# First steps of a hybrid decoder layer rearranged: weight blocks loaded ahead, a PSUM bank for each channel block, small loads on other queues

## The chip, the cores and the metric

One core of one Trainium2 chip runs the whole layer as one program. The metric is the device time of one execution in microseconds (us), lower is better. The kernel before the change takes 423.1 us (median of three runs, 421.59 to 423.76).

## What is computed

One decoder layer on 256 tokens of 1024 channels, all in float32. RWKV-7 time mixing and block attention run side by side on the same normalised input, which one combined projection `w_in` (1024 x 5408) feeds; then gates, an output projection, and a gated MLP with a causal convolution.

```python
h = rms_norm(x, norm1_g[l])
proj = h @ w_in[l]
z_rwkv, z_moba, gate_pre = ...            # 1824, 1536 and 2048 columns
z_rwkv = z_rwkv + rwkv_mu[l] * (shift_right(z_rwkv) - z_rwkv)
# inside rwkv7_time_mix:
w_log = -softplus(-(decay_bias + tanh(xw) @ w_decay_up)) - 0.5
a = sigmoid(aaa_bias + xa @ w_aaa_up)
...                                       # scan over the tokens, attention
x = x + (g_a * (y_a @ w_branch_a[l]) + g_b * (y_b @ w_branch_b[l])) @ w_out[l]
h2 = rms_norm(x, norm2_g[l])
x = x + conv_ffn(h2, w_ffn_up[l], ffn_conv_w[l], ffn_conv_b[l], w_ffn_down[l])
```

## The kernel before

**Products in three parts.** Each float32 matrix is held as a high half (`whi`, `hh`) and a remainder (`wlo`, `hl`), and a product is high x high, high x low and low x high. Weights come from memory in blocks of 512 KB: a DMA on SP's queue fills a buffer `raw`, a cast makes `whi`, a subtraction on DVE makes `wlo`. There are four `raw` buffers (`NRAW`), four of `whi` and three of `wlo`. A new block is loaded when the block four places earlier has been split (`load_next` in `split_lo`).

**The order of the work.** The first steps, function `first_steps`, stand in the order in which they are written (`manual_schedule`); what comes after is placed by a scheduler on each engine's queue. On an engine, instructions run strictly in that order. The blocks are called b0, b1, ... here, by their place in the load order: b0 and b1 are the 256 columns from 1536 on (they hold the inputs `xwa` and `xg` of the decay and gate paths), b2 the last 128 columns of that part, b3 and b4 the first half of the key projection, b5 and b6 its second half, and so on.

**The first steps.** ACT squares x, DVE scales it (`xn`), PE turns it into channel blocks by transposes into the PSUM tiles `xt`; two channel blocks share a PSUM bank. ACT takes the high half `hh` of each of the eight channel blocks (`high`), DVE the remainder `hl` (`low`). DVE casts b0, GpSimd (POOL) subtracts it, ACT casts b1 to b3, and DVE casts b4, b5 and b6. PE takes the products of b0 and b1 block by block (lines L408, L412). GpSimd issues 19 small loads (`small_loads`: parameter rows `p1`, `p2`, the matrices `wdu`, `wgu`). Between stages `keep_warm` issues products whose result nobody reads.

**The decay path.** After b0 and b1, ACT and DVE shift the result (`xwa`, L428 and L429, with the parameters `omm`), ACT takes the tanh (L447), and PE multiplies it by `wdu` into the tiles `at` and `ch` (L499), in a fixed place of its queue between the products of the projection (L266, L268 high, L271 low halves). From there a long chain of small steps leads to the transposes `prx` (L550), which need the ACT copy `rx` (L540).

**The end.** The last MLP block is added to four PSUM banks `fin[0]` to `fin[3]`, a quarter of the result each; DVE scales each and adds x (L1220), SP stores it. The last quarter goes in two halves, which both lie in `fin[3]`.

**Completion counters.** Loads issued on the queues of SP and ACT take eight completion counters in turn, `DMAHW0` to `DMAHW7`; those of GpSimd take eight others. In the lists below `[waits DMAHW3_49]` at a DMA that fills a buffer for the first time means that it is not issued until the load that used this counter last has landed.

Of the kernel before, what the change touches and what calls it, by code (L numbers as in the profile page):

```python
# [36 lines left out]
def body(tc, x, positions, norm1_g, w_in, rwkv_mu, w_decay_up, decay_bias, w_aaa_up,  # L37
# [5 lines left out]
    with ctx:  # L43
# [36 lines left out]
        def load_x():  # L80
            xs = []
            for t in range(2):
                xt = b4("x").rearrange("p a b -> p (a b)")
                for cs in (slice(0, 512), slice(512, 1024)):
                    nc.sync.dma_start(xt[:, cs], xr[t * 128:(t + 1) * 128, cs])
                xs.append(xt)
            return xs
# [6 lines left out]
        p1 = t1("p1", (51, 128))  # L94
        p2 = t1("p2", (88, 128))
# [3 lines left out]
        x_sb = load_x()  # L99
        AR = b8("AR", [128, 16, 2, 64])  # L100
        ones = cst.tile([128, 512], mybir.dt.bfloat16, name="ones")
        idle = acc("idle")

        def keep_warm(n):

            for _ in range(n):
                pe.matmul(idle, ones[:, 0:128], ones, start=True, stop=True)

# [26 lines left out]
        par = cst.tile([128, 59], F32, name="par")  # L135
        cpar = cst.tile([128, 88], F32, name="cpar")
        G1, MU, DB, AB, KK_, KA, RK, LG, LB, G2 = 0, 8, 23, 27, 31, 35, 39, 43, 47, 51
# [3 lines left out]
        def late_params():  # L141
            pt = atp("pt")
            pe.transpose(pt[:, 0:51], p1, ident[:51, :51])
            pe.transpose(pt[:, 64:152], p2, ident[:88, :88])
            dve.tensor_copy(par[:, 8:59], pt[:, 0:51])
            dve.tensor_copy(cpar, pt[:, 64:152])
            dve.tensor_scalar(omm, par[:, MU:MU + 15], -1.0, 1.0, op0=OP.mult, op1=OP.add)
            dve.tensor_scalar(omka, par[:, KA:KA + 4], -1.0, 1.0, op0=OP.mult, op1=OP.add)

        def col(i):  # L150
            return par[:, i:i + 1]
# [7 lines left out]
        for r, n in ((mu1[0:1792].rearrange("(n c) -> n c", c=128), 14),  # L159
                     (mu1[1696:1824].rearrange("(n c) -> n c", c=128), 1),  # L160
                     (rows(decay_bias, 4), 4), (rows(aaa_bias, 4), 4), (rows(k_k, 4), 4), (rows(k_a, 4), 4),
                     (rk1, 4), (rows(ln_g, 4), 4), (rows(ln_b, 4), 4), (rows(norm2_g, 8), 8)):
            loads.append((p1[at_:at_ + n], r))
            at_ += n
        loads += [(p2[0:66], conv_w[0].rearrange("w (n c) -> (w n) c", c=128)), (p2[66:88], rows(conv_b, 22)),
                  (wdu[0:64], w_decay_up[0]), (wdu[64:128], w_aaa_up[0]),
# [4 lines left out]
        loads.append((posi, positions[0].rearrange("(t p) -> p t", p=128)))  # L171

# [36 lines left out]
        def load_next(first=False):  # L209
            if queue:  # L210
                ap = queue.pop(0)
                k, c = ap.shape[1], ap.shape[2]
                raw = wp.tile([128, 1024], F32, name="raw", tag="raw", bufs=NRAW)
                rv = raw[:, :k * c].rearrange("p (k c) -> p k c", k=k)
                for ks in ((slice(0, 2), slice(2, 4)) if first else (slice(0, k),)):
                    nc.sync.dma_start(rv[:, ks], ap[:, ks])
                raws.append((raw, k, c))
# [3 lines left out]
        def split_hi():  # L221
            if raws:
                nhi[0] += 1
                eng = dve if nhi[0] in (4, 5, 6) else act
                raw, k, c = raws.pop(0)
                hi = wp.tile([128, 1024], F32R, name="whi", tag="whi", bufs=NHI)
                if eng is act:
                    act.copy(hi[:, :k * c], raw[:, :k * c])  # L228
                else:
                    eng.tensor_copy(hi[:, :k * c], raw[:, :k * c])  # L230
                halves.append((raw, hi, k, c))
# [94 lines left out]
        def first_steps():  # L326

            for i in range(NRAW):  # L330
                load_next(i == 0)
            dve.memset(ones, 1.0)
            dve.memset(eps1[:, 0:1], NORM_EPS)
            dve.memset(eps1[:, 1:2], GN_EPS)
            keep_warm(8)
            nc.scalar.dma_start(p0, rows(norm1_g, 8))
# [4 lines left out]
            small_loads(11)  # L341
# [3 lines left out]

            pts = [(chp if j < 3 else atp)("xt").rearrange("p (k t c) -> p k t c", k=2, t=2) for j in range(4)]

            def at(k):
                return pts[k // 4 * 2 + k % 2][:, k % 4 // 2]

            for t in range(2):
# [15 lines left out]
                if t == 0:  # L367
                    pt = atp("pt")
                    pe.transpose(pt[:, 0:8], p0, ident[:8, :8])
                    keep_warm(2)  # L370
                    dve.tensor_copy(par[:, 0:8], pt[:, 0:8])
                for k in (0, 2, 1, 3, 4, 6, 5, 7):
                    pe.transpose(at(k)[:, t], xn[k // 4][:, k % 4 * 128:k % 4 * 128 + 128], ident)
                if t == 0:
                    keep_warm(2)

            def high(k):
                act.activation(hh[:, k], at(k).rearrange("p t c -> p (t c)"), AF.Copy, scale=col(G1 + k))

            def low(k):  # L380
                dve.scalar_tensor_tensor(hl[:, k], at(k).rearrange("p t c -> p (t c)"), col(G1 + k),
                                         hh[:, k].bitcast(F32), op0=OP.mult, op1=OP.subtract)

            raw, k, c = raws.pop(0)
            hi = wp.tile([128, 1024], F32R, name="whi", tag="whi", bufs=NHI)
            halves.append((raw, hi, k, c))
            for k in range(6):
                high(k)
            for k in range(2):
                dve.tensor_copy(hi[:, k * 512:k * 512 + 512], raw[:, k * 512:k * 512 + 512])  # L390
                low(k)
            split_lo(pool)
            small_loads(len(loads))
            split_hi()
            high(6)
            high(7)
            for k in range(2, 8):
                low(k)
            split_lo()
            split_hi()  # L400
            p = acc()
            for b in range(2):
                w, wl = ready.pop(0)
                for k in range(4):
                    K = 4 * b + k
                    for i, xx in enumerate((hh, hl)):
                        for m in range(2):
                            pe.matmul(p[:, m * 256:m * 256 + 256], w[:, k, m * 128:m * 128 + 128], xx[:, K],  # L408
                                      start=K + i + m == 0, stop=False, skip_group_check=True)
                for k in range(4):  # L410
                    for m in range(2):
                        pe.matmul(p[:, m * 256:m * 256 + 256], wl[:, k, m * 128:m * 128 + 128],  # L412
                                  hh[:, 4 * b + k], start=False, stop=b == 1 and k == 3 and m == 1,
                                  skip_group_check=True)
            late_params()
            split_lo()
            split_hi()
# [75 lines left out]
        def chain():  # L493
# [111 lines left out]
            masks()  # L605
# [420 lines left out]
        def bulk():  # L1026
# [11 lines left out]
            rope_tables()  # L1038
# [31 lines left out]
        x_sb = load_x()  # L1070
# [13 lines left out]
        def turned(k0, k1):  # L1084

            for k in range(k0, k1, 2):
# [4 lines left out]
                for i in range(2):  # L1091
                    pk = p[:, i].rearrange("p t c -> p (t c)")
                    a = act.activation(hh[:, k + i], pk, AF.Copy, scale=col(G2 + k + i)).ins
                    d = dve.scalar_tensor_tensor(hl[:, k + i], pk, col(G2 + k + i), hh[:, k + i].bitcast(F32),
                                                 op0=OP.mult, op1=OP.subtract).ins
# [109 lines left out]
        for f, is_ in ((0, (0,)), (1, (0,)), (0, (1,)), (2, (0,)), (1, (1,)), (2, (1,)), (3, (0, 1))):  # L1205
            t, hf = divmod(f, 2)
            ts = slice(t * 128, t * 128 + 128)

            for c0, n in ((0, 512),) if f < 3 else ((0, 256), (256, 256)):
                fs = fin[f][:, c0:c0 + n]  # L1210
                cs = slice(hf * 512 + c0, hf * 512 + c0 + n)
                kw = dict(skip_group_check=True) if f == 3 else {}
                for i in is_:
                    wh, wl = ws[i]
                    pe.matmul(fs, hb[:, 0, i, ts], wh[:, 0, cs], start=False, stop=False, **kw)
                    pe.matmul(fs, hb[:, 1, i, ts], wh[:, 0, cs], start=False, stop=False, **kw)
                    pe.matmul(fs, hb[:, 0, i, ts], wl[:, 0, cs], start=False, stop=i == 1, **kw)
                if 1 in is_:
                    o = b2("o", [128, n])
                    dve.scalar_tensor_tensor(o, fs, rs[:, t:t + 1], x_sb[t][:, cs], op0=OP.mult, op1=OP.add)  # L1220
                    nc.sync.dma_start(of[t * 128:t * 128 + 128, cs], o)
# [24 lines left out]
```

## Time and profile before

| | |
|---|---|
| runs | 421.59, 423.76, 423.1 us; median 423.1 |
| the profiled execution | 422.47 us, of which the span from first to last instruction is 420.4 us |
| TensorE (PE) busy | 405.5 us, 96% of the span, mean granted clock 0.996 |
| VectorE (DVE) busy | 318.7 us, 76% |
| ScalarE (ACT) busy | 245.8 us, 58% |
| GpSimd (POOL) busy | 30.3 us, 7% |
| DMA | 70.75 MB, mean 168 GB/s |

PE, DVE, ACT and POOL are the compute engines; PEld is PE's weight load, SPq and ACTq are issues of DMAs. L266 is line 266 of the kernel. Matmuls overlap in the pipeline, so a busy PE is not a PE at its peak, and where PE waits is read from the gaps between starts. The profiled execution is 0.63 us faster than the median.

### The profile page before, as it was taken

To read this page: it belongs to the slowest core of one execution; us is meant where nothing else is said; L and a number is where in the kernel's file an instruction comes from. 1 tells how busy PE (TensorE), PEld (TensorE's weight loads), DVE (VectorE), ACT (ScalarE), POOL (GpSimd) and SP (SyncE) were. 2 spreads that over 40 slices of the span, in tenths; PEclk is the share of its full clock that TensorE was granted. 3 is DMA by queue.
4 is the path that set the end of the run, shared out by engine and by line. 5 is a ranking of instruction groups with operands and counts; after the bars stand their busy time and mean duration, and the time that the engine had idled before them with its cause. 6 is when DMAs were issued, how large, how long until landed. Compare 5 with 4: busy or idle time off the path is not lost.

```text
span 420.4 us, 8388 instructions
## 1 busy us (share of the span) xinstructions
PE 405.5 (96%) x3327; PEld 355.2 (84%) x3327; DVE 318.7 (76%) x557; ACT 245.8 (58%) x406; POOL 30.3 (7%) x48
## 2 busy tenths in 40 slices
PE   7899999999969999999999999999999999999996
PEld 3799889888868888999988888888888888888885
DVE  3697999869533796767875789879678688697793
ACT  6599745465434888785445786545455455455450
POOL 7910060000210000000000000000000000000000
PEclk9999999999998999999999999999999999999999
DMA  8776555664482244275666275755666657556512
GB/s 255 213 203 202 167 181 139 171 169 103 95 219 82 65 106 128 71 250 169 187 200 190 79 228 156 253 195 161 214 183 193 201 174 220 186 171 205 193 55 100
DMA packets 61767, 70.75 MB, mean 168 GB/s; under 512 B 8349, under 2 KB 52195, under 8 KB 61728
## 3 DMA queue, kind: packets, MB, share of 16 engines
q1 hardware_dynamic: 60768, 69.41, 55.3%
q0 software_dynamic: 944, 0.80, 0.9%
q8 instruction: 26, 0.43, 0.4%
q14 instruction: 13, 0.11, 0.1%
q10 hardware_dynamic: 16, 0.00, 0.0%
HBM read 68.76 MB, written 1.44 MB: 167 GB/s over the span
## 4 chain that ended last, share of the span: by engine, by line
PE 82%; DVE 6%; ACT 5%; issue 3%; DMA 2%; POOL 1%; SPq 0%; DVEq 0%; ACTq 0%; POOLq 0%
PE acc L1129 18%; PE acc L1134 9%; PE acc L266 7%; PE acc L271 6%; PE acc L268 6%; PE f L1151 4%; PE f L1149 4%; PE f L1153 4%; PE acc L287 4%; PE acc L291 4%; PE acc L288 4%; DVE wlo L238 2%; DMA raw<-in_w_in_dram 1%; ACT whi L228 1%; PE pgr L612 1%
## 5 line engine op out<-in xcount | busy, mean ns | idle before, releaser
L238 DVE TENSOR_TENSOR wlo<-raw,whi 128x1024 fp32r<-128x1024 f32 x124 | 152.6, 1232 | 43.9 <-PE acc L1134 12.5
L228 ACT CAST whi<-raw 128x1024 fp32r<-128x1024 f32 x121 | 127.0, 1052 | 99.7 <-PE acc L1129 37.4
L1129 PE MATMUL acc<-hx,whi 128*128 128x512 f32 x352 | 89.8, 396 | 0.0
L1129 PEld LDWEIGHTS acc<-hx,whi 128*128 128x128 f32 x352 | 63.4, 188 | 12.2
L266 PE MATMUL acc<-hx,whi 128*128 128x256 f32 x232 | 59.4, 291 | 0.0
L268 PE MATMUL acc<-hx,whi 128*128 128x256 f32 x232 | 57.1, 282 | 0.0
L1134 PEld LDWEIGHTS acc<-hx,wlo 128*128 128x128 f32 x352 | 47.0, 188 | 4.6 <-DVE wlo L238 0.6
L1134 PE MATMUL acc<-hx,wlo 128*128 128x256 f32 x352 | 47.8, 278 | 0.1
L266 PEld LDWEIGHTS acc<-hx,whi 128*128 128x128 f32 x232 | 44.2, 191 | 1.4 <-issue 0.5
L268 PEld LDWEIGHTS acc<-hx,whi 128*128 128x128 f32 x232 | 44.4, 191 | 0.4 <-issue 0.3
L271 PE MATMUL acc<-hx,wlo 128*128 128x256 f32 x232 | 36.5, 280 | 1.2 <-DVE wlo L238 1.2
L271 PEld LDWEIGHTS acc<-hx,wlo 128*128 128x128 f32 x232 | 31.1, 190 | 1.4 <-DVE wlo L238 1.4
L1151 PE MATMUL f<-whi,hb 128*128 128x512 f32 x80 | 31.2, 390 | 0.0
L1153 PE MATMUL f<-wlo,hb 128*128 128x512 f32 x80 | 31.2, 390 | 0.0
L1149 PE MATMUL f<-whi,hb 128*128 128x512 f32 x80 | 31.2, 390 | 0.0
L1139 DVE TENSOR_REDUCE an<-acc 128x256 f32<-128x512 f32 x22 | 14.3, 686 | 9.4 <-PE acc L1134 9.4
L287 PE MATMUL acc<-whi,hx 128*128 128x512 f32 x48 | 19.3, 403 | 0.0
L288 PE MATMUL acc<-whi,hx 128*128 128x512 f32 x48 | 18.8, 392 | 0.0
L1153 PEld LDWEIGHTS f<-wlo,hb 128*128 128x128 f32 x80 | 15.0, 188 | 3.2
L1151 PEld LDWEIGHTS f<-whi,hb 128*128 128x128 f32 x80 | 15.0, 188 | 2.8
L1149 PEld LDWEIGHTS f<-whi,hb 128*128 128x128 f32 x80 | 15.0, 188 | 2.8
L291 PE MATMUL acc<-wlo,hx 128*128 128x512 f32 x48 | 14.9, 393 | 0.0
(304 smaller groups left out, 630.8 us busy)
## 6 DMA issues: line engine op xcount, KB each, us to landing
raw<-in_w_ffn_up_dram SPq DMA_DIRECT2D x44, 512.0 KB, 4.1
raw<-in_w_in_dram SPq DMA_DIRECT2D x42, 512.0 KB, 4.1
raw<-in_w_ffn_down_dram SPq DMA_DIRECT2D x22, 512.0 KB, 3.4
raw<-in_w_out_dram SPq DMA_DIRECT2D x8, 512.0 KB, 3.8
x<-in_x_dram SPq DMA_DIRECT2D x8, 256.0 KB, 4.4
raw<-in_w_branch_b_dram SPq DMA_DIRECT2D x4, 512.0 KB, 3.6
raw<-in_w_branch_a_dram SPq DMA_DIRECT2D x4, 512.0 KB, 4.5
out_dram<-o SPq DMA_DIRECT2D x3, 256.0 KB, 2.0
```

What stands on the lines that cost most here:

```text
L228: act.copy(hi[:, :k * c], raw[:, :k * c])
L238: eng.tensor_tensor(lo[:, :n], raw[:, :n], hi[:, :n].bitcast(F32), op=OP.subtract)
L266: pe.matmul(om, wh[:, k, ms], xh[:, k0 + k], start=k0 + k + m == 0, stop=False, skip_group_check=True)
L268: pe.matmul(om, wh[:, k, ms], xl[:, k0 + k], start=False, stop=False, skip_group_check=True)
L271: pe.matmul(om, wl[:, k, ms], xh[:, k0 + k], start=False, stop=k0 + k == nk - 1 and m == n - 1, skip_group_check=True)
L287: pe.matmul(ps_[t], xh[:, K, ts], wh[:, k], start=K == 0, stop=False)
L288: pe.matmul(ps_[t], xl[:, K, ts], wh[:, k], start=False, stop=False)
L1129: pe.matmul(ps_[m], wh[:, k, m * 128:m * 128 + 128], hx[:, k0 + k].rearrange("p a s -> p (a s)"), start=k0 + k == 0, stop=False, skip_grou ...
L1134: pe.matmul(ps_[m][:, 0:S], wl[:, k, m * 128:m * 128 + 128], hh[:, k0 + k], start=False, stop=k0 + k == 7, skip_group_check=True)
L1149: pe.matmul(fin[f], hb[:, 0, i, ts], wh[:, 0, cs], start=st, stop=False, skip_group_check=f == 3)
L1151: pe.matmul(fin[f], hb[:, 1, i, ts], wh[:, 0, cs], start=False, stop=False, skip_group_check=f == 3)
L1153: pe.matmul(fin[f], hb[:, 0, i, ts], wl[:, 0, cs], start=False, stop=False, skip_group_check=f == 3)
```

## The change

Seven edits in the first steps and one at the end:

- Each channel block of x has a PSUM bank of its own (the last two share one), and ACT takes the high halves of six blocks, DVE of blocks 1 and 3.
- GpSimd casts b0 and makes the remainders of b0 and b1, in halves; DVE casts b1. PE takes all high products first.
- Eight weight blocks are asked for at the start: b4 to b7 get buffers of their own (`early`), and the next four calls of `load_next` do nothing.
- The small loads needed early go to ACT (two) and SP (ten), those of SP between b3 and b4 and between b4 and b5; seven stay on GpSimd, behind its splits.
- The casts of b4, b5 and b6 go from DVE to ACT.
- Five products of `keep_warm` instead of two stand ahead of the second half's transposes.
- The parameters of the MLP, `norm2_g` among them, move to `p2`, and `mlp_params` turns them late.
- The second half of the result's last quarter gets a bank of its own (`pl`); DVE adds what `fin[3]` held to x before.

```diff
-        def load_x():
+        def load_x(eng):
...
+        x_sb = load_x((nc.sync, nc.sync))
+        nc.scalar.dma_start(p0, rows(norm1_g, 8))
...
+        skipped = [0]
+        def load_next(first=False, early=False):
+            if skipped[0]:
+                skipped[0] -= 1
+            elif queue:
...
+                raw = b4("raw", (128, 1024)) if early else wp.tile([128, 1024], F32, name="raw", tag="raw", bufs=NRAW)
...
         def split_hi():
-                eng = dve if nhi[0] in (4, 5, 6) else act
+                eng = act
...
         def first_steps():
-            for i in range(NRAW):
-                load_next(i == 0)
+            for _ in range(2):
+                nc.scalar.dma_start(*loads.pop(0))
+            for i in range(2 * NRAW):
+                load_next(i == 0, early=i >= NRAW)
+                if i == 3:
+                    for n in (0, 0, 0, 0, 0, 0, 0):
+                        nc.sync.dma_start(*loads.pop(n))
+                if i == 4:
+                    for n in (0, 0, 4):
+                        nc.sync.dma_start(*loads.pop(n))
+            skipped[0] = NRAW
...
-            small_loads(11)
...
+            bk = [b("xt") for b in (chp, chp, chp, atp, atp, acc, acc)]
             def at(k):
-                return pts[k // 4 * 2 + k % 2][:, k % 4 // 2]
+                return bk[min(k, 6)][:, 0 if k < 7 else 256:256 if k < 7 else 512]
...
                 if t == 0:
-                    keep_warm(2)
+                    keep_warm(5)
...
+            parts(0, pool, False)
+            for k in (0, 1, 2, 3):
+                high(k)
+            parts(1, dve, False)
+            for k in (4, 5, 6, 7):
+                high(k)
+            parts(0, pool, True)
+            parts(1, pool, True)
+            for k in range(8):
+                low(k)
+            split_hi()
             split_hi()
...
+            for b, lo_, xx in ((0, 0, hh), (1, 0, hh), (0, 0, hl), (0, 1, hh), (1, 0, hl), (1, 1, hh)):
+                first(b, lo_, xx)
             late_params()
+            small_loads(len(loads))
...
+        mlp_params()
+        x_sb = load_x((nc.sync, nc.sync))
...
+        pl = acc()
+        xl, cl = x_sb[1], slice(768, 1024)
+        dve.scalar_tensor_tensor(xl[:, cl], fin[3][:, 256:512], rs[:, 1:2], xl[:, cl], op0=OP.mult, op1=OP.add)
...
+            fs = pl[:, 0:256] if f == 4 else fin[f][:, c0:c0 + n]
```

How it moves instructions shows at three places.

The queue of SP from the first weight block on, before: `raw` with 128x2x256 is b0 in two loads, the next three are b1, b2 and b3, and L216 with four waits is b4.

```order
L216 DMA raw<-in_w_in_dram 128x2x256 x2
L216 DMA raw<-in_w_in_dram 128x4x256
L216 DMA raw<-in_w_in_dram 128x8x128 [waits DMAHW0_49]
L216 DMA raw<-in_w_in_dram 128x4x256 [waits DMAHW1_49]
L216 DMA raw<-in_w_in_dram 128x4x256 [waits DMAHW5_49,DMAHW6_49,DMAHW2_49,Pool_49]
L216 DMA raw<-in_w_in_dram 128x4x256 [waits DMAHW3_49,DMAHW7_49,DVE_49,Activation_49]
```

The same place now, from b2 on: the first L219 is b2, the second b3, the third b4, the last one b5.

```order
L219 DMA raw<-in_w_in_dram 128x8x128 [waits DMAHW2_49]
L219 DMA raw<-in_w_in_dram 128x4x256 [waits DMAHW3_49]
L336 DMA p_70<-in_decay_bias_dram 4x128 [waits DMAHW4_49]
L336 DMA p_70<-in_aaa_bias_dram 4x128 [waits DMAHW5_49]
L336 DMA p_70<-in_rwkv_k_k_dram 4x128 [waits DMAHW6_49]
L336 DMA p_70<-in_rwkv_k_a_dram 4x128 [waits DMAHW7_49]
L336 DMA p_70<-in_rwkv_r_k_dram 4x128 [waits DMAHW0_49]
L336 DMA p_70<-in_rwkv_ln_g_dram 4x128 [waits DMAHW1_49]
L336 DMA p_70<-in_rwkv_ln_b_dram 4x128 [waits DMAHW2_49]
L219 DMA raw<-in_w_in_dram 128x4x256 [waits DMAHW3_49]
L339 DMA wdu<-in_w_decay_up_dram 64x512 [waits DMAHW4_49]
L339 DMA wdu<-in_w_aaa_up_dram 64x512 [waits DMAHW5_49]
```

Ahead of b4 there were no other loads on SP's queue; now seven small ones stand there, and b3 and b4 use the same counter, `DMAHW3`. After the two halves of `wdu` come `posi`, b5, b6 and b7, each with a wait for one of the small loads.

ACT's queue before, from the high halves to the tanh: L228 casts b1, then b2 and b3; L428 is the shift of `xwa`, L447 its tanh.

```order
L378 ACTIVATE hx<-xt,par 128x256 x6
L228 CAST whi<-raw 128x1024
L378 ACTIVATE hx<-xt,par 128x256 x2
L228 CAST whi<-raw 128x1024 x2
L418 ACT_TABLE_LOAD
L418 ACTIVATE warm<-eps_84 128x1
L428 ACTIVATE xwa<-acc,omm 128x256
L447 ACTIVATE xwa<-xwa 64x256
```

ACT's queue now: the three casts of L231 are b2, b3 and b4, the next one b5, the one behind the shift L454 is b6, and L473 is the tanh.

```order
L394 ACTIVATE hx<-xt,par 128x256 x6
L231 CAST whi<-raw 128x1024 x3
L444 ACT_TABLE_LOAD
L444 ACTIVATE warm<-eps_84 128x1
L231 CAST whi<-raw 128x1024
L454 ACTIVATE xwa<-idle,omm 128x256
L231 CAST whi<-raw 128x1024
L473 ACTIVATE xwa<-xwa 64x256
```

The casts of b4, b5 and b6 moved ahead of the tanh, b4 ahead of the table load, b5 ahead of the shift.

PE's queue before, around the products with `wdu`: L271 is the low half of b2, and L268 behind L499 opens b3.

```order
L266 MATMUL acc<-hx,whi 128x256
L271 MATMUL acc<-hx,wlo 128x256 x8
L499 MATMUL at<-xwa,wdu 128x256 x4
L499 MATMUL ch<-xwa,wdu 128x256 x4
L268 MATMUL acc<-hx,whi 128x256
```

PE's queue now, the end of the stretch ahead of the same products (L525), in which the first 13 products of b3 stand:

```order
L269 MATMUL acc<-hx,whi 128x256
L271 MATMUL acc<-hx,whi 128x256
L274 MATMUL acc<-hx,wlo 128x256 x4
L269 MATMUL acc<-hx,whi 128x256
L525 MATMUL at<-xwa,wdu 128x256 x4
L525 MATMUL ch<-xwa,wdu 128x256 x4
L271 MATMUL acc<-hx,whi 128x256
```

These 13 products (8 high, 4 low, 1 high) moved ahead of those with `wdu`; before, all of b3 stood behind them. Further on, two products of 512 columns moved from ahead of `prx` to behind it, and at the start of the MLP one cast and one subtraction stand earlier; the rest of the order is as before.

More of the change, by code (lines that the diff above doesn't have):

```diff
@@ L93, in body @@
         p0 = t1("p0", (8, 128))
-        p1 = t1("p1", (51, 128))
-        p2 = t1("p2", (88, 128))
+        p1 = t1("p1", (43, 128))
+        p2 = t1("p2", (96, 128))
         mu1 = rwkv_mu[0]
         rk1 = r_k[0].rearrange("h n -> (h n)").rearrange("(n c) -> n c", c=128)
-        x_sb = load_x()
+        x_sb = load_x((nc.sync, nc.sync))
+        nc.scalar.dma_start(p0, rows(norm1_g, 8))
+        first_low = []
         AR = b8("AR", [128, 16, 2, 64])
         ones = cst.tile([128, 512], mybir.dt.bfloat16, name="ones")
[L102 to L107, printed above, removed]
         jp = t1("jp", (128, 128), I32)
@@ L171, in body @@
         loads.append((posi, positions[0].rearrange("(t p) -> p t", p=128)))
+        loads += [(p2[0:66], conv_w[0].rearrange("w (n c) -> (w n) c", c=128)), (p2[66:88], rows(conv_b, 22)),
+                  (p2[88:96], rows(norm2_g, 8))]
         def small_loads(n):
@@ L334, in first_steps, with keep_warm @@
             dve.memset(eps1[:, 1:2], GN_EPS)
+            p = acc("idle")
+            def keep_warm(n):
+                for _ in range(n):
+                    pe.matmul(p, ones[:, 0:128], ones, start=True, stop=True)
             keep_warm(8)
-            nc.scalar.dma_start(p0, rows(norm1_g, 8))
             pool.iota(jp, pattern=[[1, 128]], base=0, channel_multiplier=-1)
@@ L374, in first_steps @@
+                for k in (0, 1, 2, 3, 4, 6, 7, 5):
+                    pe.transpose(at(k)[:, t * 128:t * 128 + 128], xn[k // 4][:, k % 4 * 128:k % 4 * 128 + 128],
+                                 ident)
                 if t == 0:
-                    keep_warm(2)
+                    keep_warm(5)
             def high(k):
-                act.activation(hh[:, k], at(k).rearrange("p t c -> p (t c)"), AF.Copy, scale=col(G1 + k))
+                if k in (1, 3):
+                    dve.tensor_scalar(hh[:, k], at(k), col(G1 + k), None, op0=OP.mult)
+                else:
+                    act.activation(hh[:, k], at(k), AF.Copy, scale=col(G1 + k))
@@ L380, in low @@
             def low(k):
[L381 to L387, printed above, removed]
-                high(k)
-            for k in range(2):
-                dve.tensor_copy(hi[:, k * 512:k * 512 + 512], raw[:, k * 512:k * 512 + 512])
+                first_low.append(dve.scalar_tensor_tensor(hl[:, k], at(k), col(G1 + k), hh[:, k].bitcast(F32),
+                                                          op0=OP.mult, op1=OP.subtract).ins)
@@ new lines, in first_steps, with parts @@
+            w = []
+            for b, eng in enumerate((pool, dve)):
+                raw, k, c = raws.pop(0)
+                hi = wp.tile([128, 1024], F32R, name="whi", tag="whi", bufs=NHI)
+                lo = wp.tile([128, 1024], F32R, name="wlo", tag="wlo", bufs=NLO)
+                w.append((raw, hi, lo))
+            def parts(b, eng, low_):
+                raw, hi, lo = w[b]
+                for i in range(2):
+                    cs = slice(512 * i, 512 * i + 512)
+                    if low_:
+                        eng.tensor_tensor(lo[:, cs], raw[:, cs], hi[:, cs].bitcast(F32), op=OP.subtract)
+                    else:
+                        eng.tensor_copy(hi[:, cs], raw[:, cs])
@@ L399, in first_steps, with first @@
+            split_lo()
             split_lo()
             split_hi()
[L401 to L409, printed above, removed]
+            def first(b, lo_, xx):
+                wv = w[b][lo_ + 1].rearrange("p (k c) -> p k c", k=4)
@@ L604, in chain @@
             yield 1.4, 4.0
-            masks()
+            with tc.issue_after(first_low[-1]):
+                masks()
             for g in range(2):
@@ L1037, in bulk @@
                 yield 0, 0.5
-            rope_tables()
+            with tc.issue_after(first_low[-1]):
+                rope_tables()
             yield from attention_input(0)
```

81 lines of the change are left out of this document (33 added, 48 removed).

## Prediction

> **What bounds the kernel now.** I read the stretches first, cut where PE starts or stops waiting (columns: length, busy time of PE, PEld, DVE, ACT and POOL, granted clock of PE, DMA share, GB/s).
>
> ```profile
> 9.35:24.07 14.72, 12.06 (x93) 10.47 (x92) 10.70 (x21) 9.71 (x20) 11.79 (x19) 1.00 0.77 213
> 24.07:122.70 98.63, 98.39 (x1116) 89.20 (x1114) 80.03 (x166) 60.73 (x96) 11.18 (x11) 1.00 0.61 163
> 122.70:127.10 4.40, 0.02 (x4) 0.02 (x3) 1.43 (x3) 1.04 (x1) 0.00 (x0) 0.97 0.83 238
> 127.10:130.20 3.10, 3.10 (x19) 3.06 (x20) 0.00 (x0) 2.04 (x5) 0.00 (x0) 0.50 0.10 31
> ```
>
> From 24.07 on PE is the bound for a hundred us: whatever makes it later or earlier there is carried on. So I read the chain that ended last from 7.95 to 24.14 (start, length, what):
>
> ```profile
> 7.95 0.43 PE idle L107 x2
> ...
> 11.02 2.40 POOL wlo L238
> ...
> 13.43 4.60 DMA raw<-in_w_in_dram
> ...
> 18.16 1.25 DVE whi L230
> ...
> 22.21 1.07 PE at L499 x8
> 23.28 0.86 PE ch L499 x8
> ...
> 25.16 0.45 PE acc L271 x4
> ```
>
> The reader sees b4: issued at 13.43 when GpSimd has freed b0's buffer, landed 4.60 us later, cast on DVE at 18.16. Behind that cast stand the parameters `omm`, for which ACT waits, as its timeline says (the arrow names what ended the wait):
>
> ```profile
> 12.64 2.05 ACT L228 CAST whi<-raw 128x1024 fp32r<-128x1024 f32 x2
> 14.70 1.28 ACT L418 ACT_TABLE_LOAD   x1
> 15.99 0.20 ACT L418 ACTIVATE warm<-eps 128x1 f32<-128x1 f32 x1
> 20.06 0.47 ACT L428 ACTIVATE xwa<-acc,omm 128x256 f32<-128x256 f32 x1 [3.86 <-DVE omka L148]
> 21.38 0.42 ACT L447 ACTIVATE xwa<-xwa 64x256 f32<-64x256 f32 x1 [0.84 <-DVE xwa L429]
> ```
>
> The products of `xwa` with `wdu` start at 22.14 and end at 24.07. Everything in the first steps counts by what it does to that moment and to the work that PE has behind it by then.
>
> **When the blocks land now.** SP's issues of b3 (with the first three loads) and of b5, each with the median time from issue to landing, and a small load on GpSimd:
>
> ```profile
> 4.10 2.49 SPq L216 DMA_DIRECT2D raw<-in_w_in_dram  x2
> raw<-in_w_in_dram SPq DMA_DIRECT2D x1, 512.0 KB, 8.6
> 15.32 0.37 SPq L216 DMA_DIRECT2D raw<-in_w_in_dram  x1
> raw<-in_w_in_dram SPq DMA_DIRECT2D x1, 512.0 KB, 6.7
> 6.88 0.52 POOL L175 DMA_DIRECT2D p<-in_rwkv_ln_b_dram  x1 [0.39 <-DMA p<-in_rwkv_mu_dram]
> ```
>
> The last load of the 4.10 row, b3, goes out at 4.65 and lands 8.6 later, at 13.25. The last row shows that a completion counter holds an issue back: GpSimd has eight of its own, and its ninth load waited for the landing of its first. On SP's queue now the load of b4 waits for `DMAHW3`, the counter of b3, so it is issued at about 13.3, not at the start; a buffer of its own brings it 0.1. With the 4.60 of the chain it lands at 17.9, where it landed at 18.03. Behind it stand the halves of `wdu` and `posi`, whose counters are those of small loads long landed; at the 0.37 of an issue, b5 goes out at 13.3 + 4 x 0.4 = 14.9. It can't land before `wdu` and itself have come through, 0.78 MB behind b4 at most at the 213 to 238 GB/s of the stretches, say 0.3 MB in a us when nothing else is under way (an estimate): 17.9 + 2.6 = 20.5. It lands at latest with the 6.7 of before, at 21.6, when `wgu` competed too. I take 21.3, nearer the measured row; b6, 0.52 MB on, at 23.0.
>
> **ACT, where the casts went.** A cast takes 2.05 / 2 = 1.03. In order: b4 17.9 to 18.95, table load to 20.2, `warm` to 20.4; wait for b5, cast 21.3 to 22.3; shift of `xwa` 0.47 to 22.8 (before it started at 20.06); DVE's shift runs beside the cast of b6, 23.0 to 24.05; tanh 0.42 to 24.5. The `wdu` products started 22.14 and now start at 24.5, end 24.5 + 1.93 = 26.4 (before 24.07). PE loses 2.4 there. The parameters `omm`, for which ACT waited 3.86, no longer matter; what is late next is b5, then b6. With b5 at its ends 20.5 and 21.6 the loss is 1.6 (b6 then at 22.2) and 2.7. DVE, freed of three casts, gains nothing that PE sees.
>
> **PE, what it has done by then.** The 13 products of b3 ahead of `wdu` take four in 0.45, 13 x 0.113 = 1.5, and come off the work behind. Net **+0.9** (0.1 to 1.2). The rest of what PE does before is covered, as its timeline shows:
>
> ```profile
> 16.40 1.07 PE L412 MATMUL acc<-hx,wlo 128*128 128x256 f32 x8
> 21.00 1.21 PE L271 MATMUL acc<-hx,wlo 128*128 128x256 f32 x8 [1.20 <-DVE wlo L238]
> ```
>
> PE ended the work of b0 and b1 at 17.4 and all but b2's low products 1.20 before 21.00, at 19.8. Now b0 and b1 end about 2.4 earlier (GpSimd's four half remainders of 1.2, from near 9.3, end near 14.1, and eight low products follow), and 0.9 of b2 and 1.5 of b3 come on top, so PE stands from 19.8 to 24.5, 4.7 us, for `xwa`. That wait covers keep_warm's three more products (0.43 / 2 x 3 = 0.65), the separate banks, the order of high products, ACT's two more issues (at SP's 0.37), GpSimd's cast of b0, which no row shows (a half on DVE takes 1.25 / 2 = 0.63, half a GpSimd remainder 1.2; I take 1.0), and the seven late small loads. If the cover went, because b4 to b6 came early, GpSimd's remainders would be the next bound.
>
> **Where it is passed on.** PE is busy 98.39 of 98.63, so no gap takes its delay back before `prx`. Two places on the chain and in the waits change it:
>
> ```profile
> 34.68 0.47 PE acc L271 x4
> 35.16 1.04 ACT whi L228
> ...
> 51.62 0.47 PE acc L291 x2
> PE prx L550 <- ACT rx L540: 0.2, 1, 0.2
> ```
>
> At 35.16 ACT's work follows PE's, so the small steps before `rx` are late by what PE is late, not by the 2.4 of the tanh. PE already waits 0.2 for `rx`; two products of 512 columns (0.47 together) move from ahead of `prx` to behind it, and that wait grows by up to as much. Between 0 and 0.47 I take **+0.3**. At the start of the MLP PE's weight load waits for a remainder that now stands earlier:
>
> ```profile
> 241.55 0.53 PEld L1134 LDWEIGHTS acc<-hx,wlo 128*128 128x128 f32 x4 [0.56 <-DVE wlo L238]
> ```
>
> Products still in flight cover about half of that wait: **-0.3**, between 0 and -0.56.
>
> **The end.**
>
> ```profile
> 414.33 1.88 DVE o L1220 x3
> 416.26 0.39 PE f L1215
> 417.27 0.48 DVE o L1220
> DVE o L1220 <- PE f L1217: 4.3, 3, 2.6
> PE f L1215 <- DVE o L1220: 0.6, 1, 0.6
> ```
>
> The last six products wait for DVE's read of their bank, until 416.2. The wait row says 0.6 from the modelled end of the product before, whose 0.28 overlap the next one's; by starts it is 0.85, from 415.4. With a bank of their own they end that much earlier; DVE is free from 416.2, and its last addition follows them at once: **-0.85** (-0.6 by the wait row alone). DVE's extra addition, 0.48, falls in the 2.6 of its longest wait for PE. SP's last issue and the store follow unchanged.
>
> **Sum.** +0.9 + 0.3 - 0.3 - 0.85 = about +0.05, on the profiled 422.47. That execution is 0.63 below the median of 423.1, so on the median's footing 423.2. About 0.5%, 2.1 us, is what a measurement of this kernel can tell from no change: this is no change.
>
> **Rivals.** *Slower, by PE's clock.* The 4.7 us of idle are longer than the 4.40 of the stretch at 122.70, behind which the granted clock was 0.50 for 3.10; the 1.20 ahead of 21.00 cost none. If the clock falls here, 3.1 x 0.5 = 1.6 come on top: 424.8, and with b5 at its late end (0.3 more, the wait 5.0) 425.1, and 425.3 with the wait for `rx` at its upper end: past 423.1 + 2.1 = 425.2, where it becomes slower than can be mistaken for no change. It decides once the wait holds whatever idle time takes the clock down, somewhere between 1.20 and 4.40. Against it: PE's products ahead may end later than 19.8, and the wait is shorter if b5 is early. I give the drop 0.35, half of it beyond the bound.
>
> The Trainium skill, page "TensorE: Matmul & The Clock Gate", section "Part 1: The HAM clock gate", says the clock is halved after an idle window of some 3.4 us, and that these windows run freely; the trace's 4.40 with a drop agrees. By that rule an idle 4.7 holds a whole window in (4.7 - 3.4) / 3.4, some 4 cases of 10, against a drop in every case if a wait as long as the 4.40 always cost one.
>
> *Faster, the loads do come early.* If no counter held b4, it would come with the blocks before it, 1.7 behind b3 (0.52 MB at 0.3), at 15.0, b5 at 16.7, b6 at 18.5. ACT then casts b4 to 16.1, b5 behind the table load and `warm` from 17.6 to 18.6, shifts to 19.1, casts b6 to 20.1, and after the tanh `wdu` starts at 20.5, 1.6 earlier; with 1.5 done ahead PE gains 3.1, and 423.1 - 3.1 + 0.3 - 0.3 - 0.85 = 419.1; with b4 merely faster than 4.60 on emptier queues it ends between that and the forecast, and with a start of `wdu` by 22.4 it is faster by more than 2.1. For it: the order lists the wait, but no trace shows it held on SP's queue. Against it: the 6.88 row, where such a wait did hold. I give it 0.22.
>
> *The edits do nothing but the end.* If b5 and b6 land at 20.5 and 22.2, PE loses only the 0.1 above, and 423.1 + 0.1 + 0.3 - 0.3 - 0.85 = 422.4; it counts as no change too.
>
> **Numbers.** Forecast's case, no clock drop or one below the bound: 0.60, 423.2, own range 422 to 424.9. Slower beyond the bound: 0.18. Faster: 0.22. The range reaches from near the early loads, 419.5, to the clock drop with a late b5 and a little, 425.4; outside I leave 2 in 10, other gaps of PE among them.
>
> **What would show it.** The changed profile should have SP's issue of b4 at 13.3 and its landing at 17.9, ACT's wait before the cast of b4 at 3 or more and before b5 near 1, the shift of `xwa` at 22 to 23, PE idle 4 to 5 us ahead of the `wdu` products, their start at 24.5, the wait for `rx` at 0.2 to 0.7, and no wait in front of the last six products. I am wrong if b4 is issued before b3 has landed, if the clock reads 0.50 behind that wait, if DVE or GpSimd and not ACT is what `wdu` waits for, or if the 4.40 gap at 122.70, which no edit touches, changes its length.

## The result, and the profile after

The changed kernel takes 427.64 us (median of five, 425.41 to 428.34) against 423.12 (421.59 to 424.08) in the same comparison: 1.0106 times as long, 95% interval 1.0083 to 1.0129. A second comparison gave 1.0104 (1.0074 to 1.0135). It is slower by 4.2 to 4.5 us; forecast was 423.2, no change, with a range up to 425.4.

The profiled execution took 425.41, 2.94 more than that of before. Its stretches around the two places where PE stands idle longest (columns as in the prediction: length, busy times, granted clock, DMA share, GB/s):

```profile
20.84:25.37 4.53, 0.27 (x4) 0.07 (x2) 1.72 (x4) 2.84 (x5) 0.67 (x2) 0.99 1.07 343
25.37:28.97 3.60, 3.60 (x17) 2.62 (x17) 2.75 (x15) 2.96 (x9) 0.00 (x0) 0.54 1.10 356
126.10:130.30 4.20, 0.10 (x12) 0.00 (x1) 1.53 (x3) 1.04 (x1) 0.00 (x0) 0.68 0.84 238
130.30:133.40 3.10, 3.10 (x22) 3.06 (x22) 0.00 (x0) 2.04 (x5) 0.00 (x0) 0.50 0.19 61
```

PE waits 4.53 us in front of the `wdu` products, which start at 25.37 (before 22.14); waits of PE are given from start to start, so they hold the product ahead of them. Behind the wait the clock reads 0.54, and the 16 products take 3.53 until the next one starts at 28.90 (before 1.93). The gap near 126 is the one of 122.70, about as long as it was. The chain of waits into the first of these (start, length, what) names the cause of the wait:

```profile
4.67 8.01 DMA raw<-in_w_in_dram
12.70 0.40 SPq L219
15.02 0.46 SPq L219
15.53 8.32 DMA raw<-in_w_in_dram
23.95 1.04 ACT whi L231
25.00 0.33 ACT xwa L473
25.37 2.08 PE at L525 x8
27.45 1.52 PE ch L525 x8
```

b3, issued at 4.67, lands at 12.68, and only then, at 12.70, is b4 issued. b5 goes out at 15.02 behind the three small loads (the halves of `wdu` and `posi`), and b6 at 15.53; b6 lands at 23.85, ACT casts it, and the tanh and PE follow. ACT's timeline has both late blocks in front of the path (the arrow names what ended the wait):

```profile
16.83 1.05 ACT L231 CAST whi<-raw 128x1024 fp32r<-128x1024 f32 x1 [3.07 <-DMA raw<-in_w_in_dram]
22.20 1.04 ACT L231 CAST whi<-raw 128x1024 fp32r<-128x1024 f32 x1 [2.81 <-DMA raw<-in_w_in_dram]
23.15 0.47 ACT L454 ACTIVATE xwa<-idle,omm 128x256 f32<-128x256 f32 x1
23.95 1.04 ACT L231 CAST whi<-raw 128x1024 fp32r<-128x1024 f32 x1 [0.33 <-DMA raw<-in_w_in_dram]
24.91 0.41 ACT L473 ACTIVATE xwa<-xwa 64x256 f32<-64x256 f32 x1
```

Before, the shift of `xwa` started at 20.06 and nothing but DVE's parameters held it. Now b4, b5 and b6 are cast in front of the tanh, and ACT, which runs in order, waits 3.07 for the first, 2.81 for the second and 0.33 for the third.

At the end, the last products have a tile of their own (`acc`) and no wait:

```profile
418.89 0.28 PE L1248 MATMUL f<-wlo,hb 128*128 128x256 f32 x1
419.01 0.28 PE L1246 MATMUL acc<-whi,hb 128*128 128x256 f32 x1
419.93 0.48 DVE L1251 SCALAR_TENSOR_TENSOR o<-acc,rs,x 128x256 f32<-128x256 f32 x1 [0.23 <-PE acc L1248]
```

The first of the last six follows the product ahead of it by 0.12; before, 0.86 lay between them (415.40 to 416.26).

A second profile of the same kernel, 426.72 us, shows what varies from one execution to the next:

```profile
21.64:26.27 4.63, 0.15 (x3) 0.01 (x1) 2.01 (x5) 2.84 (x5) 0.69 (x2) 1.00 1.07 341
26.27:30.00 3.73, 3.73 (x18) 2.66 (x19) 2.46 (x12) 3.46 (x10) 0.00 (x0) 0.56 1.08 353
```

`wdu` starts another 0.9 later, and the clock falls again.

### The profile page after: what moved, and what is told of

The parts are those of the page before. It is cut to its first block, busy times and chain, and to the rows that moved or that the text cites. A ratio compares the mean times of both kernels' runs of the same rounds, so it can differ in the third digit from the quotient of the medians.

```text
span 423.4 us, 8398 instructions
## 1 busy us (share of the span) xinstructions
PE 406.8 (96%) x3330; PEld 357.2 (84%) x3330; DVE 319.2 (75%) x556; ACT 247.0 (58%) x406; POOL 26.6 (6%) x41
## 4 chain that ended last, share of the span: by engine, by line
PE 87%; DMA 5%; ACT 3%; DVE 2%; issue 1%; SPq 1%; ACTq 0%
PE acc L1158 19%; PE acc L1163 10%; PE acc L269 7%; PE acc L274 7%; PE acc L271 7%; PE acc L290 4%; PE acc L294 4%; PE f L1180 4%; PE acc L291 4%; PE f L1182 4%; PE f L1178 4%; DMA raw<-in_w_in_dram 4%; ACT sc L976 1%; PE pgr L639 1%; ACT whi L231 1%
## 5 line engine op out<-in xcount | busy, mean ns | idle before, releaser
L231 ACT CAST whi<-raw 128x1024 fp32r<-128x1024 f32 x123 | 129.1, 1051 | 111.1 <-PE acc L1158 42.4
L241 DVE TENSOR_TENSOR wlo<-raw,whi 128x1024 fp32r<-128x1024 f32 x123 | 149.7, 1219 | 49.6 <-PE acc L1163 12.5
L271 PE MATMUL acc<-hx,whi 128*128 128x256 f32 x232 | 57.3, 282 | 0.0
L271 PEld LDWEIGHTS acc<-hx,whi 128*128 128x128 f32 x232 | 44.3, 191 | 0.6 <-issue 0.5
```

What stands on the lines that cost most here:

```text
L241: eng.tensor_tensor(lo[:, :n], raw[:, :n], hi[:, :n].bitcast(F32), op=OP.subtract)
L271: pe.matmul(om, wh[:, k, ms], xl[:, k0 + k], start=False, stop=False, skip_group_check=True)
```

## The experiments

The changed kernel unaltered, for the second profile:

> The changed kernel once more, unaltered, for a second profile and a tighter comparison. Theory (the late wdu products and the clock): 427 to 428 in most executions, wdu starting at 25 to 26 and the granted clock below 0.6 in their stretch; what is more than the 2.9 us of the first profile comes from the length of the two waits and the phase of the clock, so a second profile differs from the first in the stretches 20 to 32 and 120 to 140 and nowhere else by over 0.3. Rival (a stage later in the program is slower too): the two profiles and that of before differ by over 0.5 somewhere behind 150.

427.01 us. The stretch near 26 is shown above; PE is 0.9 later there than in the first profile, and 0.3 later where the gap near 126 begins (126.34 against 126.02), since in the first profile products of 256 columns went 0.118 apart between 29 and 45, in this one and in before 0.113. The gap, which no edit touches and for which the profile names no releaser, is 5.03 long against 4.28, and with the longer half clock behind it the distance is 1.3 from 146 on and stays so (160.04 and 161.41, 171.12 and 172.44). So the difference lies where the theory puts it, but for the pace of those products. What the executions at 428 had more was not profiled.

**Is it the counter that holds b4?** The seven rows of parameters go to GpSimd's queue, so that no load stands between b3 and b4:

```diff
                 if i == 3:
-                    for n in (0, 0, 0, 0, 0, 0, 0):
-                        nc.sync.dma_start(*loads.pop(n))
+                    late = loads[:7]
+                    del loads[:7]
...
+            for a in late:
+                nc.gpsimd.dma_start(*a)
```

> The changed kernel with its seven rows of parameters issued on GpSimd's queue, not on SP's ahead of b4: b4 then no longer takes the counter that b3 has. Theory (the counter holds b4 back, and with it everything that ACT casts ahead of the tanh): b4 is issued before 7 and lands near 15 in place of 16.8, b5 near 17.5 in place of 22.2, the wdu products start at 20.5 to 21.5 in place of 25.4, PE has no wait over 1.5 us there and the clock stays at 1.00 behind it; the time falls by 4 + 1.7 = 5 to 6 us below the changed kernel, to 421 to 423. Rival (memory, not the counter, sets when b4 to b6 land): b5 lands no earlier than 21, wdu starts at 24 or later, and the time stays within 1.5 us of the changed kernel.

421.20 us, 0.9957 of before (0.9937 to 0.9978), 6.4 less than the changed kernel. ACT's casts of b4 to b6 and its tanh, then PE's products, then one stretch:

```profile
15.20 1.06 ACT L231 CAST whi<-raw 128x1024 fp32r<-128x1024 f32 x1 [1.12 <-DMA raw<-in_w_in_dram]
17.68 1.04 ACT L231 CAST whi<-raw 128x1024 fp32r<-128x1024 f32 x1
18.94 1.05 ACT L231 CAST whi<-raw 128x1024 fp32r<-128x1024 f32 x1 [0.23 <-DVE omm L140]
21.51 0.42 ACT L475 ACTIVATE xwa<-xwa 64x256 f32<-64x256 f32 x1 [0.78 <-DVE xwa L457]
21.98 1.13 PE L527 MATMUL at<-xwa,wdu 64*128 64x256 f32 x8
22.95 1.03 PE L527 MATMUL ch<-xwa,wdu 64*128 64x256 f32 x8
11.90:47.40 35.50, 35.46 (x291) 34.12 (x291) 29.53 (x61) 30.57 (x50) 10.14 (x18) 1.00 0.67 201
```

b4 can be cast at 15.20, and ACT no longer waits for the landing of b5 or b6. `wdu` starts at 21.98, PE is busy 35.46 of 35.50 us around it, at the full clock. Of the theory's numbers only `wdu` came 0.5 later than stated, with the tanh at 21.51. One move of seven small loads turns the change from 1.1% slower into 0.4% faster.

The counter, or the time that seven issues take on SP? Three of the rows stay ahead of b4, four go behind it:

```diff
                 if i == 3:
-                    for n in (0, 0, 0, 0, 0, 0, 0):
+                    for n in (0, 0, 0):
                         nc.sync.dma_start(*loads.pop(n))
                 if i == 4:
-                    for n in (0, 0, 4):
+                    for n in (0, 0, 0, 0, 0, 0, 4):
```

> The changed kernel with three of the seven rows ahead of b4 on SP's queue and four behind it: b4 then takes the counter of b0's first half, and b5 takes the one that b4 has. Theory (it is the counter, not the seven issues, that holds a block): b4 is issued at 7.5 to 8 and lands near 15, and now b5 is not issued before b4 has landed, so b5 still lands at 20 to 22 and wdu starts at 23.5 to 25.5; the wait has moved from the cast of b4 to that of b5, and the time falls by less than 2 us, some 1.7 more where the clock holds. Rival (the time that seven small issues take on SP holds b4): with four of them behind b4, b5 comes as much earlier as b4, 2 us, wdu starts at 23 and PE waits 2.2; the time falls by 3.5 or more.

427.26 us, 1.0100 of before (1.0066 to 1.0133). SP's issues of b4 and of b5 with b6, ACT's casts of b4, b5, b6, and PE's wait and what follows:

```profile
9.00 0.40 SPq L219 DMA_DIRECT2D raw<-in_w_in_dram  x1
15.40 1.02 SPq L219 DMA_DIRECT2D raw<-in_w_in_dram  x2
14.73 1.05 ACT L231 CAST whi<-raw 128x1024 fp32r<-128x1024 f32 x1 [0.43 <-DMA raw<-in_w_in_dram]
21.07 1.05 ACT L231 CAST whi<-raw 128x1024 fp32r<-128x1024 f32 x1 [3.77 <-DMA raw<-in_w_in_dram]
24.12 1.04 ACT L231 CAST whi<-raw 128x1024 fp32r<-128x1024 f32 x1 [1.63 <-DMA raw<-in_w_in_dram]
21.48:25.54 4.06, 0.15 (x3) 0.00 (x1) 2.01 (x5) 2.43 (x5) 0.60 (x1) 0.85 1.09 350
25.54:29.00 3.46, 3.46 (x16) 2.54 (x16) 2.45 (x12) 2.82 (x8) 0.00 (x0) 0.50 1.09 355
```

As the theory has it, b4 comes 2.1 earlier and that gains nothing: b5 is issued at 15.40 all the same, and the wait has moved from the first cast to the second (3.07 and 2.81 became 0.43 and 3.77). What holds b5 is again a counter, but not the one that was expected. b4's had come back by 14.73, when b4 is cast. It is the last of the four rows behind b4 that now takes the counter of b3:

```profile
13.24 0.25 SPq L339 DMA_DIRECT2D p<-in_rwkv_ln_b_dram  x1
```

It goes out at 13.24, when b3 has landed and is cast, and holds what stands behind it on SP's queue, the halves of `wdu`, `posi` and b5. b4 itself was not what bound the path; the blocks after it were. (b4's issue, at 9.00, was 1 us later than expected.)

**What makes b5 land late?** Between the landing of b4 and that of b5 lie 5.4 us. In the changed kernel's 16.8 to 20.0, and then its 20.0 to 22.2, the two kinds of queue shared the DMA engines (packets, MB, share of 16 engines):

```profile
q1 hardware_dynamic: 748, 0.50, 56.6%
q0 software_dynamic: 119, 0.32, 38.2%
q1 hardware_dynamic: 557, 0.55, 75.7%
q0 software_dynamic: 127, 0.10, 27.1%
```

The first of each pair is SP's queue, the second GpSimd's seven small loads, `wgu` first. Together 1.47 MB came through, where `wdu` and b5 are 0.78. GpSimd's loads are moved behind its constants:

```diff
-            small_loads(len(loads))
             act.activation(warm, eps1[:, 0:1], AF.Sigmoid)
             late_consts()
+            small_loads(len(loads))
```

> The changed kernel with the seven small loads of GpSimd (0.37 MB in all) issued behind its constants, about 4 us later. Theory (they share the DMA engines with b5, which landed 5.4 us behind b4 where 2.5 was enough for its bytes and wdu): b5 lands at 20 to 20.5 in place of 22.2, b6 at 22, wdu starts at 23.5, the wait of PE is 2.7 and the clock holds; the time falls by 2 + 1.7 = 3 to 4 us. Rival (SP's late issue alone sets b5's landing, 7.1 us behind it as before the change): b5 lands at 22 and the time stays within 1 us.

423.48 us, 1.0027 of before (1.0003 to 1.0051), 4.2 less than the changed kernel. ACT's casts of b5 and b6, PE's wait and what follows, and the one queue that moved data between 17.5 and 21.4:

```profile
21.37 1.04 ACT L231 CAST whi<-raw 128x1024 fp32r<-128x1024 f32 x1 [1.31 <-DMA raw<-in_w_in_dram]
22.87 1.05 ACT L231 CAST whi<-raw 128x1024 fp32r<-128x1024 f32 x1
21.45:24.29 2.84, 0.15 (x3) 0.00 (x1) 1.47 (x2) 2.75 (x5) 1.25 (x3) 1.00 1.14 362
24.29:27.00 2.71, 2.71 (x22) 2.25 (x23) 2.54 (x14) 2.41 (x7) 0.00 (x0) 1.00 1.02 289
q1 hardware_dynamic: 1288, 1.26, 102.2%
```

b4 was cast only at 17.49 here, and yet b5 follows 3.9 later in place of 5.4 (4.5 in the second profile of the changed kernel), b6 with no wait, and the wait of PE is 2.84, behind which the clock stays at 1.00. The theory holds, with a smaller gain in the landing (21.3 against the 20 to 20.5 expected) and the full gain in time, as in the profile the clock's fall went with the wait. It need not go in every execution: the profiled one, 422.54, is the fastest of twelve, and five took 424.5 to 426.6 at a mean granted clock of 0.986 to 0.988, where the profiled one has 0.992. Nor are GpSimd's loads all that b5 shares the engines with: 1.26 MB of SP's own queue passed in those 3.9 us, so packets of the blocks behind b5, which SP issues right after it, came through ahead of its last ones. The Trainium skill (page "DMA: Bandwidth & Descriptors", section "Queues, rings and completion order") says that each DMA engine takes turns between its queues packet by packet; the 38% for 0.32 MB beside 57% for 0.50 MB show both queues served at once and not one going first, but not the turns themselves.

**Is the slow stretch behind the wait the clock's?** Sixteen products that nobody reads are put ahead of the `wdu` products; the scheduler then moves the 13 products of b3 behind them:

```diff
+            for _ in range(16):
+                pe.matmul(pw[0][0], ones[:, 0:128], ones, start=True, stop=True)
             for ct in range(4):
```

> The changed kernel with 16 products of 512 columns whose result nobody reads ahead of the wdu products; the scheduler then puts the 13 products of b3 behind them. Theory (PE's clock fell in the wait of 4.5 us and cost 1.7): PE is busy until about 23 and idle for 2.5, the granted clock in the wdu products is 1.00 in place of 0.54, these take 1.9 in place of 3.6; b3's 13 products cost 1.5 behind them, so the time stays within 0.5 us of the changed kernel while the wdu products end 1.7 earlier. Rival (the wdu products are slow for another reason, such as their weights): they take 3.6 again and the time rises by 1.5.

427.23 us, 1.0109 of before (1.0078 to 1.0140).

```profile
23.42:25.74 2.32, 0.16 (x2) 0.01 (x1) 1.96 (x5) 1.42 (x3) 0.00 (x0) 1.00 1.10 358
25.74 1.13 PE L527 MATMUL at<-xwa,wdu 64*128 64x256 f32 x8 [2.16 <-ACT xwa L473]
26.70 1.03 PE L527 MATMUL ch<-xwa,wdu 64*128 64x256 f32 x8
```

Idle for 2.32 in place of 4.53, PE keeps its clock, and the same products with the same weights take 1.9 in place of 3.5. So the 1.6 is the clock's. The time is unchanged, since b3's 1.5 now comes behind.

**Do the casts belong on ACT?** The casts of b4 to b6 go back to DVE, in the changed kernel and in the version with the rows on GpSimd:

```diff
-                eng = act
+                eng = dve if nhi[0] in (3, 4, 5) else act
```

> The changed kernel with the casts of b4, b5 and b6 on DVE as before. Theory (ACT's casts, in front of the shift and the tanh, are what the late blocks delay): the blocks land as late as in the changed kernel (b4 16.8, b5 22.2), but the shift of xwa waits only for DVE's parameters behind the cast of b4, at 20 to 20.5; wdu starts at 22 to 22.5, the wait of PE is 1.5 or less with clock 1.00 behind it, and the time falls by 4 to 5 us, to 422.5 to 424. Rival (not the casts but the late blocks themselves bind PE): PE waits as long for b4's products, and the time falls by less than 1.5.

The first of the two: 424.71 us, 1.0046 of before (1.0021 to 1.0070). It gains 2.9, not the 4 to 5 of the theory, and the theory's step failed: the scheduler put the cast of b5 in front of DVE's half of the shift. DVE's two, then PE's wait and what follows:

```profile
23.11 0.69 DVE L233 CAST whi<-raw 128x1024 fp32r<-128x1024 f32 x1 [3.98 <-DMA raw<-in_w_in_dram]
23.72 0.48 DVE L455 SCALAR_TENSOR_TENSOR xwa<-idle,par,xwa 128x255 f32<-128x255 f32 x1
20.82:24.70 3.88, 0.16 (x2) 0.00 (x0) 1.59 (x4) 0.47 (x2) 0.92 (x2) 1.00 1.05 348
24.70:27.60 2.90, 2.90 (x17) 2.05 (x18) 2.87 (x18) 2.35 (x7) 0.00 (x0) 0.71 1.11 350
```

The late block binds on whichever engine its cast stands in front of the path; with b6's cast out of the way PE starts 0.7 earlier, although b5 landed 0.9 later than in the changed kernel. The rival (b4's own products bind PE) is not what the rows show. The twelve executions fall apart: four took 422.65 to 423.04 at a mean granted clock of 0.992 to 0.996, eight, the profiled one among them, 424.2 to 427.0 at 0.982 to 0.988.

> The version with the rows on GpSimd's queue, with the casts of b4, b5 and b6 on DVE as before. Theory (the casts on ACT cost something only behind late blocks; with early blocks PE is the bound): wdu starts between 20.5 and 22, PE has no wait there, the time is within 0.5 us of 421.2. Rival (a cast ahead of the tanh always costs what it takes): the time differs by 1 us or more.

The second: 420.41 us, 0.9939 of before (0.9919 to 0.9959). With early blocks `wdu` starts at 21.36 without a wait. The medians differ by 0.8 from the version with the casts on ACT, in different comparisons whose intervals overlap; whether the casts' place is worth something with early blocks stays open.

**The end.** The last edit alone on the kernel before, and taken out of the version just told:

> The kernel before with the last edit alone, a bank of its own for the second half of the last quarter. Theory: the last six products start behind the ones before them, 0.85 earlier, and the time falls by 0.7 to 0.9, to 422.2. Rival (the end is set by the store or DVE's added operation): within 0.2 of before, whatever PE does.

> The version with the rows on GpSimd's queue and the casts of b4 to b6 on DVE, with the end as it was before the change (both halves of the last quarter in one bank). Theory (the bank of its own is worth what the last six products start earlier, less 0.3 that the last store gives back): 0.4 to 0.6 slower than with the new end, 420.9. Rivals: 0.85 slower, 421.3, if nothing is given back; no difference, within 0.2, if the store sets the end.

422.45 us, 0.9989 of before (0.9972 to 1.0006), and 420.67 us, 0.9948 (0.9929 to 0.9967), against 0.9939 with the new end. Both differences are about 0.4, neither clear of zero by itself, and neither rules out the 0.85 or nothing at all. The profiles say more. In that of the changed kernel the last six products start 0.74 earlier against the product ahead of them (0.12 for 0.86), and DVE's last addition follows their first by 0.92 in place of 1.01, so DVE wins 0.83, and the profiles of the two runs here agree (0.12 between the products with the new end, 0.86 with the old). From the end of DVE's last addition to the end of the span it is 3.0 us (423.4 less 420.41) where it was 2.65 (420.4 less 417.75). These 0.34 are not given back by the new end, as the second run's theory had it: before with the new end has 2.7 there, and the version with the old end 2.9. They come with the other edits; what causes them is not shown.

**The version from here.** In the first steps PE still waits for the second half of b1's cast on DVE, 0.72 by the row below. That half goes to ACT:

```diff
-            parts(1, dve, False)
+            parts(1, dve, False, (0,))
             for k in (4, 5, 6, 7):
                 high(k)
+            parts(1, act, False, (1,))
```

> The version with the rows on GpSimd's queue and the casts of b4 to b6 on DVE, and the second half of b1's cast on ACT in place of DVE. There DVE takes 1.0 for each half of b1 beside GpSimd's subtractions, where a half took 0.43 with GpSimd idle, and PE waits 0.9 for the second. Theory (DVE is slowed by GpSimd's work on the same memory, ACT is not): ACT's half takes 0.55 to 0.65, PE's wait near 11.5 shrinks from 0.9 to 0.5 or less, and as PE is the bound from there on the time falls by 0.4 to 0.6, to 419.9. Rival (the wait is passed on to b2's cast on ACT or to the wdu products): the wait near 11.5 shrinks but another appears, and the time stays within 0.2.

419.84 us, 0.9925 of before (0.9904 to 0.9946): the lowest median of all. The cast on DVE and PE's wait in the version before it, then the cast on ACT and PE's waits here:

```profile
10.47 1.51 DVE L416 CAST whi<-raw 128x512 fp32r<-128x512 f32 x1
12.13 1.08 PE L438 MATMUL idle<-hx,whi 128*128 128x256 f32 x7 [0.72 <-DVE whi L416]
11.32 0.65 ACT L416 CAST whi<-raw 128x512 fp32r<-128x512 f32 x1
12.03 1.20 PE L441 MATMUL idle<-hx,whi 128*128 128x256 f32 x8 [0.23 <-ACT whi L416]
21.02 1.14 PE L530 MATMUL at<-xwa,wdu 64*128 64x256 f32 x8 [0.59 <-ACT xwa L478]
```

The expected "1.0 for each half" was a mean of unlike halves, 0.46 and 1.51. The wait shrank from 0.72 to 0.23, but another of 0.59 appeared ahead of `wdu`: part of the gain is passed on, as the rival says, and 0.6 between two comparisons whose intervals overlap does not decide between them.

## Why the prediction was wrong

**b4 and its counter: right.** "Issued at about 13.3, not at the start": 12.70. Landing 17.9 with the chain's 4.60: 16.8, with 4.1.

**b5 and b6: the step that failed first.** "I take 21.3", between 20.5 and 21.6, and b6 at 23.0. b5's issue was right (14.9, measured 15.02; 15.59 in the second profile), the landings were 22.2 and 23.85, in the second profile 21.9 and 24.8, outside the ends. What was mis-sized is what passes ahead of them: "0.78 MB behind b4 at most" and "0.52 MB on" are 1.3 MB, and from the landing of b4 to that of b6 2.1 MB came through (1.47 up to b5, 0.63 behind it) in 7.0 us, in the second profile 2.2 MB in 7.4, where the forecast had 5.1. The rate is the 0.3 MB in a us of the estimate. The rest is 0.42 MB of GpSimd's loads, which the experiment on them shows to count, and nearly 0.4 MB of SP's queue, on which b7 and more blocks went out from 16.1 on. The 6.7 of before could not bound this: in the time from b5's issue to its landing 1.6 MB passed there, and 2.0 here. `wdu` so started at 25.37, in the second profile at 26.27, in place of 24.5. Net of b3's products, 1.5, PE lost 1.7 and 2.6, not 0.9.

**The wait of PE: right by luck.** 4.7 was forecast, 4.53 and 4.63 were measured: PE stood from 20.84, not 19.8, and `wdu` was late by about as much. The work of b0 and b1 ended at 16.4, not at 15.0, because it was not GpSimd's remainders that set its end but PE's own 36 products from 11.71 on, behind the wait of 0.72 for DVE's cast.

**The clock: the step that decides.** The drop had a chance of 0.35 and so stayed out of the sum. It came in both profiles of the changed kernel. The price was right (1.6; the 16 products took 3.53 for 1.93). Of all profiles here the idle stretches of PE up to 2.84 us left the clock at 1.00, and each one from 3.88 on, those at `wdu` as well as the gap near 120 to 127 in every version, brought half the clock, within it or up to 1.2 us behind it. "It decides once the wait holds whatever idle time takes the clock down, somewhere between 1.20 and 4.40" was right, and a wait longer than the one row that shows a drop should have been taken to drop. The rule of the Trainium skill (page "TensorE: Matmul & The Clock Gate", section "Part 1: The HAM clock gate"), by which a free-running window of 3.4 us must be idle, was read as 4 cases of 10 and made the drop look less likely than the row did. That the windows run freely agrees: in each profile the changes of the clock lie whole multiples of 3.41 us apart (in the changed kernel down at 25.24, up at 28.65, down at 127.64, up at 134.47, which is 1, 29 and 2 of them). That a whole window must be idle does not: at `wdu` the clock fell behind windows in which PE was idle for 2.2, 2.7, 3.0 and 3.4 of the 3.41 us (the waits of 3.88, 4.06, 4.63 and 4.53), and held behind one with 1.9 (the wait of 2.84). By these rows an idle 4.7, which leaves at least 2.35 to one of two neighbouring windows, would have cost the clock every time, and one of 2.84 can cost it or not, by where it lies. At the gap near 126 even less was enough: 1.1 us of idle behind some 180 products of 32x16, in the version with early blocks and the casts on DVE.

**The other terms.** `prx`: no wait is left there in the changed kernel, as PE is later than ACT's `rx`, so it was -0.2 and not +0.3. The start of the MLP: the wait before it is gone, -0.28 for -0.3. The end: -0.83 at DVE as forecast, but behind it 0.34 more passes, which comes with other edits, so that "the store follow unchanged" failed and -0.5 of -0.85 was kept.

**The sum again**, for the second profile, whose 426.72 lies near the median and 4.25 above before's: `wdu` +4.1, clock +1.7, b3 -1.5 and `prx` -0.2 make 4.1, and 3.9 is what PE is late by at 90 us; the gap near 126 and the half clock behind it +1.0; MLP -0.3; end -0.5: 4.3. In the first profile `wdu` is +3.2, the slower pace +0.7, the gap and its clock +0.1. The slower rival named the right mechanism and was priced from too early a landing: with the measured `wdu` it gives 423.1 + 1.7 + 1.6 - 0.3 - 0.5 = 425.6, just past the range, and with that of the second profile 426.5. The faster rival had the direction of the change without the counter, but not its size, as the version with the rows on GpSimd shows: 421.2, where it gave 419.1, with `wdu` at 21.98 and not 20.5.

## What to carry to other kernels

An early request is only as early as the completion counter that it needs: count how many loads are issued between a large block and the one eight places on, and put small loads on a queue with counters of its own. Even a small load that takes the counter of a block on its way holds up everything behind it on its queue. What a block shares the DMA engines with is all that is issued before it lands, the blocks behind it too, not only what was issued ahead of it. A cast that waits for memory must not stand in front of a small step that a whole engine waits for, on any engine. Where a wait of PE is longer than one that has already cost it the clock, put the clock's price into the sum, not beside it.

## What was not expected of the hardware

DVE's cast of 128x512 took 1.51 us while GpSimd was subtracting (10.47 to 11.98), 0.46 for the half ahead of it and 0.42 in the kernel before. GpSimd subtracts beside both halves: its first subtraction ends at 10.27 and its second at 11.69, each 0.28 or 0.29 ahead of the end of a cast, and so it is in the changed kernel (9.85 and 11.27, the casts at 10.13 and 11.56). A cast looks as if it waited for the subtraction under way. DVE's multiply-adds of 128x256 on PSUM tiles took 0.47 each beside the subtractions and 0.48 with GpSimd idle, so they were not slowed. The Trainium skill (page "GPSIMD Engine Reference", section "1. Specifications") says that GpSimd shares its memory interface with DVE, for DVE instructions that use both ports or have two SBUF inputs; the multiply-adds with their one SBUF input agree, and the casts do if they use both ports, which no row shows. No run here varied that alone.

The clock fell up to 1.2 us after PE had taken up work again (24.70 to 25.9 in the changed kernel with its casts on DVE), so the end of a wait is not the end of its danger. Products of 256 columns kept one pace in one execution and another in the next, 0.113 or 0.118 apart at a granted clock of 1.00 in both; what sets it was not tried.
